# Seven products in place of eight for the pooling, gate, branch and output projections of a trunk layer

## The chip, the cores and the metric

The kernel runs on one core of a Trainium2 chip. The metric is device time in microseconds (us) of one execution; several executions are timed and their median is given. A hardware profile of one further execution gives the trace.

## The reference

One layer over 2048 latent tokens of width 1024, with 256 context tokens that serve as extra keys and values. All tensors are float32.

```python
q, k, v, p, gt = _split_proj(_modulate(x, sh1, sc1) @ w_in[l])   # 1024 q, 256 k, 256 v, 512 pool, 2048 gate columns
attn_o = _banded_attention(q, k, v, k_c, v_c, attn_sink[l])
# _merge_branches:
attn_d = attn_o @ w_ab                                           # 1024 x 1024
pooled = _multiscale_pool(p)                                     # centred means over 2/4/8/16 tokens, minus the token
pool_d = jnp.einsum('blgc,gcd->blgd', pooled, w_pool).reshape(B, L, D_MODEL) * pool_scale
merged = jax.nn.sigmoid(g_attn) * attn_d + jax.nn.sigmoid(g_pool) * pool_d
y = merged @ w_out                                               # 1024 x 1024
x = _layernorm(ALPHA * x + g1 * y, ln1_g[l], ln1_b[l])
u = _modulate(x, sh2, sc2)
h = jnp.square(jax.nn.relu(u @ w1)) @ w2                         # 1024 x 4096, 4096 x 1024
x = _layernorm(ALPHA * x + g2 * h, ln2_g[l], ln2_b[l])
```

## The kernel before

TensorE (PE) multiplies in a fast float32 format with fewer bits. A float32 operand is therefore split in two: ScalarE (ACT) casts the high part and VectorE (DVE) subtracts it to get the low part (`split`, two lines: L59 and L62). A product is three matmuls, high by high, high by low and low by high, so a tile of 512 columns costs three 128x512 matmuls for each 128 rows of depth.

The kernel has these stages, one after the other:

- **Attention**, to about 872 us: 64 units (16 blocks of 128 tokens, 4 key heads), with the q, k and v projections of later blocks filled in between. The modulated input `u` is spilled to DRAM (`u_scr`), the attention output to `a_scr`. In the last two blocks `early_pool` fills PE with two of the pooling projections.
- **The middle**, 872 to about 1762 us. The tokens are taken in two halves `c` of 1024. For each half come the pooling projections (`p_group`), the means (`p_finish`, `pool_gate`), the 16 gate tiles (`ps_gp`, `ps_ga`), the attention branch (`ps_ab`), the merge, the output projection (`out_mm`, `ps_out`, matmuls of 256 columns), the first layer norm and the transposes of the second input (`u2_half`). These products are plain: eight blocks of 128 depth, all columns. Gates, means and merged values stay in SBUF. `ada_next` spreads the late modulation vectors (`adacc`) over the first half.
- **MLP up**, 1762 to about 2390 us: 32 items (`Pair`), each 256 weight columns for 1024 tokens, computed by Strassen's scheme in its Winograd form: seven products (1, 6, 2, 7, 5, 4, 3) of 12 matmuls each, with sums of weight blocks on GpSimd (POOL), sums of the results on DVE from PSUM, and sums for the next product on POOL. The weight parts are split into `R` tiles seven steps ahead, in eight slots. The left operands (`La`, `Lb`) stay for 16 items.
- **MLP down**, 2390 us to the end, with seven products over the whole depth (`ps_y`).

PE's order is written out by hand (`tc.manual_schedule`); the other engines get their order from a scheduler that works through the program with its own estimates. All transfers are issued by SyncE's queue (SP), in order: a transfer that waits for its data holds up those behind it.

Of the kernel before, what the change touches and what calls it, by code (L numbers as in the profile page):

```python
# [36 lines left out]
def block_kernel(  # L37
# [7 lines left out]
    if u_scr is None:  # L45
        u_scr = tc.dram_tile([P, KT, T], F32, name="u_scr")
        a_scr = tc.dram_tile([P, KT, T], F32, name="a_scr")
    x1_scr = tc.dram_tile([T, D], F32, name="x1_scr")
    g2_scr = tc.dram_tile([D], F32, name="g2_scr")
    us_scr = [tc.dram_tile([P, 7, 4, 512], F32, name=f"us_scr{c}") for c in range(2)]  # L50
    hs_scr = [[tc.dram_tile([P, 4, 16, P], F32, name=f"hs_scr{c}{p}") for p in range(7)] for c in range(2)]
# [55 lines left out]
    rpx = ExitStack()  # L107
    rp = rpx.enter_context(sbuf("right", side="right"))
# [4 lines left out]
    def raw_tile(shape):  # L113
        return rp.tile(shape, F32, name="raw", tag="raw", bufs=2)
# [8 lines left out]
    wk = [(rp.tile([P, 4, 512], F32R, name="wkh", tag="raw", bufs=2), wkp.tile([P, 4, 512], F32R, name=f"wkl{h}"))  # L123
# [436 lines left out]
    UP = (0, 344, 688)  # L560

    def load_u(xs, u0, uu, pieces=1):

        def step(kk):
            raw = raw_tile([P, 2, UW])
            sp.dma_start(raw, u_scr[:, 2 * kk:2 * kk + 2, u0:u0 + UW])
            for k in range(2):
                uh = slot(xs, 0, [P, UW], F32R, "uh2")
                ul = slot(xs, 1, [P, UW], F32R, "ul2")
                for z in [slice(i, i + UW // pieces) for i in range(0, UW, UW // pieces)]:  # L570
                    split(uh[:, z], ul[:, z], raw[:, k, z])
                uu.append((uh, ul))
        return [lambda kk=kk: step(kk) for kk in range(4)]

    uu0 = []
    early = []

    def early_pool(g):

        def begin():  # L580
            raw = big.tile([P, KT, P], F32, name="w1", tag="x", bufs=1)
            sp.dma_start(raw, w_in_r[:, :, 1536 + g * P:1536 + (g + 1) * P])
            both = twp.tile([P, 2, KT, P], F32R, name="w1s", tag="w1s", bufs=1)
            w.extend((both[:, 0], both[:, 1]))
            split(*w, raw)
            pt = ptp.tile([P, PW], F32, name="pt1", tag="pt1", bufs=2)
            pool.memset(pt[:, 0:8], 0.0)
            early.append(pt)

        def step(i, k):  # L590
            if k == 0:
                box[i] = ps512("ps_p", "proj")[:, 0:344]
            wh, wl = w
            uh, ul = (t[:, UP[i]:UP[i] + 344] for t in uu0[k])
            pe.matmul(box[i], wh[:, k, :], uh, start=k == 0, stop=False)
            pe.matmul(box[i], wh[:, k, :], ul, start=False, stop=False)
            pe.matmul(box[i], wl[:, k, :], uh, start=False, stop=k == KT - 1)
            if k == KT - 1:
                act.copy(early[g][:, 8 + UP[i]:8 + UP[i] + 344], box[i])
        box, w = {}, []  # L600
        return [[begin]] + [u for i in range(3) for u in [[lambda i=i, k=k: step(i, k)] for k in range(KT)] + [[]]]
# [11 lines left out]
    for n, (b, g) in enumerate(order):  # L613
# [24 lines left out]
        if (b, g) == (NB - 3, 1):  # L638
            wkx.close()
            ptx = ExitStack()  # L640
            ptp = ptx.enter_context(sbuf("pooled", side="right"))
            twp = at.enter_context(sbuf("tailw", side="right"))
            lu = load_u(RA, 0, uu0, 3)
        if (b, g) == (NB - 3, 2):
            lu[0]()
# [79 lines left out]
    for c in range(2):  # L725
# [16 lines left out]
        if c:  # L742
            w_first = wcols(w_in, 1536)
# [225 lines left out]

# [344 lines left out]
```

## Time and profile before

| | before |
|---|---|
| median of 3 runs | 3038.16 us (3036.88 to 3038.42) |
| the profiled execution's own time | 3039.96 us |
| its span, first to last instruction | 3038.2 us |
| PE busy | 2909.0 us (96%) |
| DVE, ACT, POOL busy | 1819.1, 1369.1, 1380.6 us |
| bytes moved | 395.38 MB |

The busy share of PE is an average. The windows by stage and the waits are read first, the groups of instructions next: the first tell where PE stands idle, the second what one instruction of each kind takes. Matmuls overlap, so the time for one is the busy time of a group divided by its count, not the mean duration.

### The profile page before, as it was taken

What the parts mean: (1) busy time and instruction counts of PE and PEld (TensorE: products, weight loads), DVE (VectorE), ACT (ScalarE), POOL (GpSimd) and SP (SyncE); (2) the same over time, 40 slices, a digit from 0 to 9 for tenths busy, and PEclk for the clock granted to TensorE, in tenths of its full rate; (3) what the DMA queues carried; (4) which work ended last, traced back from release to release, by engine and by line L of the source; (5) the groups of instructions that cost most, each with busy time, mean ns of one, the idle gap of its engine ahead of it and who ended that gap; (6) DMA issues with size and microseconds to landing.
All of it is one profiled execution on the core that took longest, in us unless ns stands there. A gap on an engine that the chain in (4) does not pass through costs nothing. (4 is left out here: it accounts for less than half of the span.)

```text
span 3038.2 us, 42601 instructions
## 1 busy us (share of the span) xinstructions
PE 2909.0 (96%) x15336; PEld 2481.3 (82%) x15336; DVE 1819.1 (60%) x3201; ACT 1369.1 (45%) x2462; POOL 1380.6 (45%) x1638
## 2 busy tenths in 40 slices
PE   8899999999899999899999779999999799999998
PEld 5789989998888888888889668888888587888886
DVE  5577877877875444742144775557555453556675
ACT  3477767777741131432121455556555332333342
POOL 1867777777540014423032556657665240123244
PEclk9999999999999999999999889999999899999999
DMA  7111111112234433342122475547554684566563
GB/s 255 35 32 37 32 37 31 38 42 61 67 100 144 127 125 111 112 144 78 56 97 84 141 263 161 153 149 222 156 153 124 246 308 153 187 215 218 196 209 108
DMA packets 343015, 395.38 MB, mean 130 GB/s; under 512 B 16785, under 2 KB 277009, under 8 KB 341010
## 3 DMA queue, kind: packets, MB, share of 16 engines
q1 hardware_dynamic: 342802, 392.64, 40.5%
q8 instruction: 121, 1.98, 0.3%
q14 instruction: 92, 0.75, 0.1%
HBM read 275.13 MB, written 117.44 MB: 129 GB/s over the span
## 5 line engine op out<-in xcount | busy, mean ns | idle before, releaser
L1220 PE MATMUL ps_y<-La,R 128*128 128x512 f32 x2688 | 619.4, 393 | 25.8 <-ACT R L59 12.1
L1220 PEld LDWEIGHTS ps_y<-La,R 128*128 128x128 f32 x2688 | 508.9, 190 | 136.4 <-ACT La L59 13.7
L1039 PE MATMUL ps_h<-La,R 128*128 128x512 f32 x2112 | 485.2, 390 | 0.3 <-ACT cx L1044 0.3
L1039 PEld LDWEIGHTS ps_h<-La,R 128*128 128x128 f32 x2112 | 397.2, 188 | 83.3 <-ACT cx L1044 0.7
L62 DVE TENSOR_TENSOR R<-hraw,R 128x512 fp32r<-128x512 f32 x224 | 198.0, 890 | 150.7 <-ACT R L59 150.2
L59 ACT CAST R<-hraw 128x512 fp32r<-128x512 f32 x224 | 137.6, 621 | 281.3 <-PE ps_y L1220 272.9
L62 DVE TENSOR_TENSOR pl<-ps_pt,ph 128x512 fp32r<-128x512 f32 x312 | 212.5, 686 | 70.5 <-ACT ph L59 68.6
L465 POOL TENSOR_SCALAR s<-s,sm 128x640 f32<-128x640 f32 (+1 forms) x256 | 201.6, 795 | 103.0 <-DVE sm L464 53.9
L462 ACT ACTIVATE s<-s,sm 128x641 f32<-128x641 f32 (+1 forms) x256 | 209.8, 820 | 70.2 <-DVE sm L456 69.8
L456 DVE CUSTOM_DVE_ANT_0 s<-ps_s,mask,nsink 128x640 f32<-128x640 f32 (+1 forms) x256 | 211.5, 863 | 29.8 <-PE ps_s L451 29.7
L59 ACT CAST ph<-ps_pt 128x512 fp32r<-128x512 f32 x312 | 179.3, 580 | 109.3 <-PE ps_pt L486 106.0
L861 POOL TENSOR_TENSOR sa<-sa,m 128x512 f32<-128x512 f32 x32 | 57.1, 1805 | 374.5 <-DVE sa L860 374.5
L486 PE MATMUL ps_pt<-ident,s 128*128 128x128 f32 x1248 | 189.7, 274 | 12.4 <-DVE pl L62 8.2
L62 DVE TENSOR_TENSOR R<-sraw,R 128x512 fp32r<-128x512 f32 x160 | 146.3, 917 | 77.3 <-ACT R L59 76.8
L59 ACT CAST wh<-raw 128x2048 fp32r<-128x2048 f32 (+1 forms) x38 | 67.0, 1771 | 276.1 <-DMA raw<-w_in 73.6
L486 PEld LDWEIGHTS ps_pt<-ident,s 128*128 128x128 f32 x1248 | 151.6, 141 | 43.1 <-DVE pl L62 11.3
L62 DVE TENSOR_TENSOR wl<-raw,wh 128x2048 fp32r<-128x2048 f32 (+1 forms) x38 | 86.3, 2274 | 159.5 <-ACT wh L59 159.5
L59 ACT CAST R<-sraw 128x512 fp32r<-128x512 f32 x160 | 98.9, 621 | 155.2 <-PE ps_h L1039 97.5
L1039 PE MATMUL ps_h<-Lb,R 128*128 128x512 f32 x576 | 139.5, 396 | 25.4 <-ACT Lb L59 21.9
L1039 PEld LDWEIGHTS ps_h<-Lb,R 128*128 128x128 f32 x576 | 109.8, 191 | 49.7 <-ACT Lb L59 22.3
L66 PE MATMUL ps_out<-wh,mg 128*128 128x256 f32 x512 | 143.1, 281 | 0.0
L67 PE MATMUL ps_out<-wl,mg 128*128 128x256 f32 x512 | 142.8, 280 | 0.0
(264 smaller groups left out, 7098.4 us busy)
## 6 DMA issues: line engine op xcount, KB each, us to landing
hraw<-hs_scr SPq DMA_DIRECT2D x112, 512.0 KB, 4.0
w<-w_mlp_out SPq DMA_DIRECT2D x72, 512.0 KB, 5.4
sraw<-w_mlp_in SPq DMA_DIRECT2D x64, 512.0 KB, 6.3
hs_scr<-s SPq DMA_DIRECT2D x96, 256.0 KB, 4.6
raw<-w_in SPq DMA_DIRECT2D x19, 1024.0 KB, 5.5
raw<-w_ada SPq DMA_DIRECT2D x16, 1024.0 KB, 5.3
rw<-us_scr SPq DMA_DIRECT2D x14, 1024.0 KB, 5.4
raw<-u_scr SPq DMA_DIRECT2D x8, 1032.0 KB, 5.5
```

Source lines behind the costliest of these rows:

```text
L59: act.copy(hi, src)
L62: (lo_eng or dve).tensor_tensor(lo, src, hi.bitcast(F32), ALU.subtract)
L66: pe.matmul(ps, sh, mh, start=first, stop=False)
L67: pe.matmul(ps, sh, ml, start=False, stop=False)
L456: dve.tensor_tensor_reduce(out=s[:, 0:n], in0=pieces[z][2], in1=mk[z], op0=ALU.add, op1=ALU.min, scale=-1.0 / math.sqrt(HD), scalar=nsink[ ...
L462: act.activation(s[:, 0:n + 1], s[:, 0:n + 1], AF.Exp, bias=sm[:, 0, j:j + 1], scale=-1.0, accum_out=sm[:, 1, j:j + 1])
L465: pool.tensor_scalar(s[:, 0:n], s[:, 0:n], sm[:, 2, j:j + 1], 1.0, ALU.mult, ALU.mult)
L486: pe.transpose(pt[:, c:c + P], self.s.probs[2 * z + j][:, o:o + P], ident)
L861: pool.tensor_tensor(s, s, m0[j][:, a:a + m], ALU.add)
L1039: pe.matmul(ps, a, b, start=p in (1, 6, 5) and k == 0 and i == 0, stop=k == 3 and i == 2, skip_group_check=p not in (1, 6, 5))
L1220: pe.matmul(ps, a, b, start=n == 0 and z == 0, stop=n == 15 and z == 2)
```

## The change

The four projections of the middle are computed by the same seven products as the MLP. The two halves of the depth and the two halves of the tile's rows or columns are the blocks. Everything after attention is one stream of 68 items of seven products: 20 items of pooling and gate columns (10 for each half of the tokens), 8 of the branch (`BranchCols`), 8 of the output projection (`Rows`, one for 256 tokens) and 32 of the MLP up (`HiddenCols`). The MLP down stays as it is, but for the names of its buffers.

- Six items have their products 1 and 2 computed early, in the last two attention blocks (`Tail`, `NX = 6`), in place of `early_pool`.
- The sums of the left operand are made beside the stream as jobs: `act_sums` loads 1 MB, makes four sums and stores them (four times for each half of `u` and of `a`; on POOL for the first, on DVE for the other three). `w_out_planes` does it for the output weights. The means are 16 jobs of 512 tokens (`pool_job`).
- Gates, means and merged values no longer stay in SBUF: each result goes to DRAM (`p_scr`, `sa_scr`, `sp_scr`, `mp_scr`, `ms_scr`) and is loaded again. A branch tile loads its gate and its mean through a ring of three tiles (`ldring`), a left operand its raw planes through another ring of three (`rwring`).
- The first layer norm of the second half of the tokens (`ln1_late`) and the last four of the modulation sums run beside the first half of the MLP up.
- The `R` tiles are split five steps ahead, in six slots, where it was seven and eight.

```diff
-    UP = (0, 344, 688)
...
+    def act_sums(scr, sums, c, kk, e, raw, new):
+
+        sp.dma_start(raw, scr[:, 2 * kk:2 * kk + 2, c * CH:(c + 1) * CH])
+        v = raw.rearrange("p k (b r t) -> p k r b t", r=2, t=P)
+        a11, a12, a21, a22 = v[:, 0, 0], v[:, 1, 0], v[:, 0, 1], v[:, 1, 1]
+        s1, s2 = (new().rearrange("p (b t) -> p b t", t=P) for _ in range(2))
+        e.tensor_tensor(s1, a21, a22, ALU.add)
+        e.tensor_tensor(s2, s1, a11, ALU.subtract)
+        e.tensor_tensor(a21, a11, a21, ALU.subtract)
+        e.tensor_tensor(a12, a12, s2, ALU.subtract)
+        for p, t in ((5, s1), (6, s2), (7, a21), (3, a12)):
+            sp.dma_start(sums[c][:, SPL[p], kk].rearrange("p (b t) -> p b t", t=P), t)
...
-            pending += early_pool(0) + early_pool(1)
+            pending += tail.steps()
...
-    w_first = wcols(w_in, 1792, pieces=4)
...
-        if c == 0:
-            pooled = [p_finish(early[g], g) for g in range(2)]
-            for g in (2, 3):
-                pooled.append(p_finish(p_group(w_first, g), g))
...
+    rring = mpa.ring(6 * 4096, name="R")
+    rawring = mb.ring(3 * 8192, name="sraw")
+    rwring = mb.ring(3 * 2048, name="rw")
+    extring = mb.ring(4 * 2048, name="ext")
+    string = mb.ring(10 * 2048, name="st")
+    PQ = 512 + 16
+    ldring = gp_[0].ring(3 * 2048, name="ld")
+    pjring = gp_[0].ring(4 * PQ * 4, name="pj")
...
+            for k in range(4):
+                raw = rwring.tile([P, 512], F32, name="rw")
+                s = self.src(p)[:, k]
+                sp.dma_start(raw if len(s.shape) == 2 else blocks(raw), s)
+                t = ltile(p, k)
+                split(t[:, 0], t[:, 1], raw)
+                self.L[p].append(t)
...
+            ps = self.X if p in (1, 2) else self.Z if p in (5, 3) else self.Y
+            r = self.R.pop(p)
+            first = p in (1, 6, 5)
+            for k in range(4):
+                m = self.stage.L[p][k]
+                mm = ((r[:, 0, k], m[:, 0]), (r[:, 0, k], m[:, 1]), (r[:, 1, k], m[:, 0]))
...
+    class BranchCols(Cols):
...
+        def fin(self, key, ps, t):
+            r, h = rn(key)
+            s, m = ldtile("sa"), ldtile("mp")
+            sp.dma_start(blocks(s), tok_dst(sa_scr, 2 * self.n + h, self.c, r))
+            sp.dma_start(blocks(m), tok_dst(mp_scr, 2 * self.n + h, self.c, r))
+            if t is None:
+                t = sttile("c11")
+                dve.tensor_tensor(t, ps, s, ALU.mult)
+            else:
+                dve.tensor_tensor(t, ps, t, ALU.add)
+                dve.tensor_tensor(t, t, s, ALU.mult)
+            (dve if key in (11, 12) else pool).tensor_tensor(t, t, m, ALU.add)
+            combine(key, t, self.got, self.put)
...
+    for kk in range(4):
+        job(2 * kk, ada, kk)
+        job(2 * kk + 1, sums, u_scr, us1, 1, kk)
+        job(9 + kk, w_out_planes, kk)
+    for n, (z, g, q) in enumerate((z, g, 2 * z + q) for z in range(2) for g in range(4) for q in range(2)):
+        job(12 + n // 2, pool_job, g, q)
+    for kk in range(4):
+        job(13 + kk // 2 * 2, sums, a_scr, as1, 0, kk)
+        job(17 + kk // 2 * 2, sums, a_scr, as1, 1, kk)
+    for k in range(8):
+        job(8 + 2 * k, ada, 4 + k)
...
+    seq = [(p, i) for g in groups for p in ORDER for i in g if not (items[i].early and p in (1, 2))]
+    AHEAD = 5
...
+        items[i].prod(p)
+        if i + 1 in cuts:
+            items[i + 1].stage.fill(p)
+        if n + AHEAD < len(seq):
+            q, j = seq[n + AHEAD]
+            items[j].prep(q)
```

What the change does to the order is shown at two places of the branch stage. In the rows, `raw`, `sraw` and `rw` are loaded tiles; `R`, `La`, `av`, `mg` and `wl` are split parts; `sa` is a gate, `mp` a weighted mean; `c_`, `cx`, `cu`, `cv` are results of an item. SP's queue before, at the start of the first half's branch:

```order
L667 DMA raw<-w_in 128x8x256 [waits DMAHW5_49,DVE_49]
L667 DMA raw<-w_ab 128x8x256 [waits DMAHW7_49,DMAHW0_49,DVE_49]
L842 DMA raw<-a_scr 128x2x1024 [waits DMAHW6_49,DVE_49]
L842 DMA raw<-a_scr 128x2x1024 [waits DMAHW0_49,DVE_49]
L964 DMA g_scr<-gb_11461 1x1024 [waits DVE_49]
L842 DMA raw<-a_scr 128x2x1024 [waits DMAHW1_49,DVE_49]
```

SP's queue now, in the first half's branch:

```order
L930 DMA ms_scr_73<-cv 512x1x128 [waits Pool_49]
L935 DMA sa<-sa_scr 128x4x128 [waits DMAHW6_49,DMAHW3_49]
L936 DMA mp<-mp_scr 128x4x128 [waits DMAHW1_49,DVE_49]
L935 DMA sa<-sa_scr 128x4x128 [waits DMAHW7_49,DMAHW5_49,Pool_49]
L936 DMA mp<-mp_scr 128x4x128 [waits DMAHW3_49,DVE_49]
L930 DMA ms_scr_73<-s_15513 512x1x128 [waits Pool_49]
L847 DMA sraw<-w_ab 128x4x256 [waits DMAHW0_49,DVE_49]
L847 DMA sraw<-w_ab 128x4x256
L935 DMA sa<-sa_scr 128x4x128 [waits DMAHW4_49,DMAHW2_49,Pool_49]
L936 DMA mp<-mp_scr 128x4x128 [waits DMAHW5_49,DVE_49]
```

Loads of gates and means, loads of weights and stores of results now alternate on the one queue; a gate's load waits for the slot that POOL or DVE frees, and a store for its sum on POOL. DVE before, in the same stage:

```order
L62 TENSOR_TENSOR av<-raw,av 128x512 [waits Activation_49]
L62 TENSOR_TENSOR wl<-raw,wh 128x2048 [waits DMAHW6_49,Activation_49]
L860 TENSOR_TENSOR sa<-ps_ab,sa 128x512 [waits PE_49] x2
L62 TENSOR_TENSOR mg<-sa,mg 128x512 [waits Activation_49] x2
L860 TENSOR_TENSOR sa<-ps_ab,sa 128x512 [waits PE_49] x2
L62 TENSOR_TENSOR wl<-raw,wh 128x2048 [waits DMAHW7_49,Activation_49]
```

DVE now, in the second half's branch:

```order
L943 TENSOR_TENSOR c_16212<-c_16212,mp 128x512 [waits DMAHW2_49,DVE_49]
L68 TENSOR_TENSOR La<-rw,La 128x512 [waits DMAHW1_49,Activation_49]
L941 TENSOR_TENSOR cv<-ps_16259,cv 128x512 [waits PE_49]
L68 TENSOR_TENSOR R<-sraw,R 128x512 [waits Activation_49]
L942 TENSOR_TENSOR cv<-cv,sa 128x512 [waits DMAHW4_49,DVE_49]
L941 TENSOR_TENSOR cv<-ps_16283,cv 128x512 [waits PE_49]
L68 TENSOR_TENSOR R<-sraw,R 128x512 [waits DMAHW6_49,Activation_49]
L941 TENSOR_TENSOR cx<-ps_16137,cx 128x512 [waits PE_49]
L68 TENSOR_TENSOR La<-rw,La 128x512 [waits DMAHW0_49,Activation_49]
```

Sums from PSUM (`ps_`), low parts for the running item, low parts for the next stage and the gate's multiply now share DVE, and the multiply waits for a transfer.

## Rows read from the trace of the kernel before

**Rows 1.** The page: busy time by engine, and the span in 40 slices

```profile
PE 2909.0 (96%) x15336; PEld 2481.3 (82%) x15336; DVE 1819.1 (60%) x3201; ACT 1369.1 (45%) x2462; POOL 1380.6 (45%) x1638
PE   8899999999899999899999779999999799999998
DVE  5577877877875444742144775557555453556675
PEclk9999999999999999999999889999999899999999
DMA  7111111112234433342122475547554684566563
```

**Rows 2.** Windows by stage: length, busy time (count) by engine, clock, DMA share, GB/s

```profile
400.00:760.00 360.00, 358.77 (x2441) 326.65 (x2440) 288.16 (x671) 259.54 (x553) 273.60 (x530) 1.00 0.15 41
800.00:872.00 72.00, 68.84 (x527) 67.00 (x525) 50.22 (x120) 52.85 (x114) 31.44 (x56) 1.00 0.07 16
872.00:1762.00 890.00, 840.23 (x4544) 725.16 (x4544) 431.82 (x743) 237.19 (x344) 241.11 (x169) 0.97 0.36 118
1762.00:2390.00 628.00, 614.39 (x2688) 506.99 (x2688) 357.75 (x409) 331.37 (x537) 373.35 (x251) 0.99 0.54 165
2390.00:2420.00 30.00, 19.12 (x55) 13.07 (x56) 16.95 (x20) 15.79 (x21) 0.39 (x1) 0.72 1.03 396
```

**Rows 3.** Waits of PE, longest first: us in total, times, longest

```profile
PE ps_h L1039 <- ACT Lb L59: 21.9, 1, 21.9
PE ps_y L1220 <- ACT R L59: 12.1, 1, 12.1
...
PE ps_u L929 <- ACT xn L900: 11.2, 3, 5.0
```

**Rows 4.** Groups of PE matmuls: shape, count | busy us, mean ns | idle before

```profile
L1220 PE MATMUL ps_y<-La,R 128*128 128x512 f32 x2688 | 619.4, 393 | 25.8 <-ACT R L59 12.1 <-ACT La L59 11.3 <-DVE La L62 2.3
...
L66 PE MATMUL ps_out<-wh,mg 128*128 128x256 f32 x512 | 143.1, 281 | 0.0
...
L685 PE MATMUL ps_gp<-uh,wh 128*128 128x512 f32 x256 | 102.2, 399 | 0.0
...
L685 PE MATMUL ps_p<-uh,wh 128*128 128x344 f32 x144 | 44.6, 334 | 3.2 <-ACT wh L59 1.7 <-ACT uh L59 1.5
...
L929 PE MATMUL ps_u<-ident,xn 128*128 128x128 f32 x128 | 25.0, 330 | 20.6 <-ACT xn L900 11.2 <-ACT u2f L930 9.3
...
L595 PE MATMUL ps_p<-uh,w1s 128*128 128x344 f32 x48 | 15.9, 332 | 0.0
```

**Rows 5.** DVE in order of time in the MLP up: start us, duration us

```profile
1798.57 0.68 DVE L1057 TENSOR_TENSOR cv<-ps_h,cv 128x512 f32<-128x512 f32 x1
1799.17 1.18 DVE L62 TENSOR_TENSOR R<-sraw,R 128x512 fp32r<-128x512 f32 x1
1800.27 0.68 DVE L1057 TENSOR_TENSOR cv<-ps_h,cv 128x512 f32<-128x512 f32 x1
1800.87 1.18 DVE L62 TENSOR_TENSOR R<-sraw,R 128x512 fp32r<-128x512 f32 x1
```

**Rows 6.** POOL in order of time, the same stretch

```profile
1798.06 1.74 POOL L1020 TENSOR_TENSOR sraw<-sraw,ext 128x512 f32<-128x512 f32 x1
1799.76 1.74 POOL L1010 TENSOR_TENSOR ext<-sraw,ext 128x512 f32<-128x512 f32 x1
```

**Rows 7.** POOL's sums of weight blocks in the MLP up: min/median/max ns

```profile
L1010 POOL TENSOR_TENSOR ext<-sraw,ext x29: 1277/1287/1752, 1799.8 to 2317.1; 128x512 f32<-128x512 f32 x29
```

**Rows 8.** DMA issues: count, KB each, median us from issue to landing

```profile
hs_scr<-s SPq DMA_DIRECT2D x96, 256.0 KB, 4.6
...
adaw<-w_ada SPq DMA_DIRECT2D x16, 512.0 KB, 8.1
...
x<-x_scr SPq DMA_DIRECT2D x32, 256.0 KB, 3.7
```

More of the change, by code (lines that the diff above doesn't have):

```diff
@@ L575, in block_kernel @@
[L575 to L601, printed above, removed]
+    ORDER = (1, 6, 2, 7, 5, 4, 3)
@@ new lines, in block_kernel @@
+    items = []
+    w_ab_v, w1v = weight_cols(w_ab), weight_cols(w_mlp_in)
+    for c in range(2):
+        stage = Stage(act_planes(u_scr, us1, c), tail.L if c == 0 else None)
+        for i in (0, 1, 2, 3, 4, 5, 6, 7, 8, 9) if c == 0 else (0, 1, 6, 7, 8, 9, 2, 3, 4, 5):
+            it = (PoolCols if i < 2 else GateCols)(stage, c, i, w_in_v, U_COLS[i])
+            it.early = c == 0 and i < NX
+            if i >= 2:
+                it.g, it.dst = (i - 2) % 4, sa_scr if i < 6 else sp_scr
+            items.append(it)
@@ new lines, in block_kernel @@
+    job(20, lambda: tc.keep_in_program_order(act.preload_act_table_set(EXP_LN)))
+    job(28, to_rows)
+    for z in range(4):
+        job(37 + 2 * z, ln1_late, 4 + z)
+        job(46 + 2 * z, ada, 12 + z)
+    cuts = [i for i in range(1, len(items)) if items[i].stage is not items[i - 1].stage]
+    groups, i = [], 0
+    while i < len(items):
+        two = i + 1 < len(items) and items[i].stage is items[i + 1].stage and (i == 0 or i in cuts or i + 2 in cuts)
+        groups.append(list(range(i, i + 1 + two)))
+        i += 1 + two
@@ new lines, in block_kernel @@
+    seq = [(p, i) for g in groups for p in ORDER for i in g if not (items[i].early and p in (1, 2))]
+    AHEAD = 5
+    items[0].load()
+    items[1].load()
+    items[0].stage.fill(6)
+    for n in range(AHEAD):
+        p, i = seq[n]
+        items[i].prep(p)
+        items[0].stage.fill(p)
+    for p in ORDER:
+        items[0].stage.fill(p)
+    at_step = {}
+    for g in groups:
+        steps = [n for n, (_, i) in enumerate(seq) if i in g]
+        for z, i in enumerate(g):
+            at_step.setdefault(steps[z * len(steps) // len(g)], []).append(i)
@@ new lines, in block_kernel @@
+    for i in (0, 1):
+        items[i].begin()
+    for n, (p, i) in enumerate(seq):
+        for f in [f for d, f in ends if d == 0]:
+            f()
+        ends[:] = [(d - 1, f) for d, f in ends if d]
+        for j in at_step.get(n, ()):
+            ahead = [g for g in groups if g[0] == j + 1]
+            for i2 in ahead[0] if ahead else ():
+                items[i2].load()
+                items[i2].begin()
+            for f in jobs.get(j, ()):
+                f()
+        items[i].prod(p)
[4 more added lines that the diff above has]
+            items[j].prep(q)
```

875 lines of the change are left out of this document (459 added, 416 removed).

## The prediction

> **What bounds the kernel now.** I read the page's busy line first, then windows by stage, then PE's waits, then single rows for prices. PE is busy 2909.0 of 3038.2 us [rows 1], so time is PE's work plus the little it waits. By stage [rows 2]: the end of attention is full (68.84 of 72 us), the middle has 840.2 of 890, the MLP up 614.4 of 628. The long waits are single events at stage starts: 21.9 and 12.1 us, and 11.2 in three [rows 3]. The other engines have room in the middle: DVE 432 of 890, ACT 237, POOL 241, DMA share 0.36 at 118 GB/s. So fewer matmuls there come off the time one for one, until something else fills: the question is what the change asks of DMA and DVE in a shorter middle.
>
> **What PE saves.** A 512-column matmul costs 619.4/2688 = 0.2304 us [rows 4]. In units of that, the middle had 3 x 768 = 2304 for the gates and the branch (one group of 256 of the nine stands in [rows 4]), 432 pooling matmuls of 344 columns = 290, and 1536 output matmuls of 256 columns = 768 (one group of three stands for each): 3362, or 775 us. Now there are 240 products: six items with five, 14 gate items with seven, 16 branch and output items with seven. At 12 matmuls each that is 2880, or 664 us. Saved: 111. Half of the 128 transposes `ps_u` (25.0 us, [rows 4]) leaves for the MLP up: 12 more. If nothing but PE limits the stream, the middle's length S is 840 - 111 - 12 = 717 us.
>
> **What is added outside the middle.**
> - End of attention: 6 items x 2 products x 12 = 144 matmuls of 512 columns replace 144 of 344 (three groups of 48, one stands in [rows 4]). That is 144 x 0.2304 x (1 - 344/512) = 11 us, and it counts, since PE is full there. The 16 sums on POOL (16 x 1.287 = 21 us, [rows 7]) hide under POOL's 31 of 72 [rows 2]; without that cover they would cost up to 21.
> - Opening of the stream: its first weight loads stand on SP behind attention's last stores, then come a load (3.7 to 8.1 us, [rows 8]), two POOL sums and a split. I take 12 us, nearest to load plus sums plus split. Bounds: 2, were it prefetched, and 21.9, the longest stage start of [rows 3].
> - MLP up: four pieces of layer norm, half the transposes, four modulation pieces, and `R` five steps ahead instead of seven. The transposes are 12 us of PE, but 13.6 us of idle in that stage (628 - 614.4) takes part of it: +8, bounds 0 and 25 (twice the transposes). MLP down: 0, its matmuls and rings keep their sizes.
>
> **What the middle now asks of DMA.** Gates, means, merged values and the sums of the operands go through DRAM. By the shapes of the diff, in MB: weights, gate stores and early reloads of the 20 items 43; sums of `u` 8 and of `a` 17; output-weight planes 12; pooling jobs 22; modulation weights 13; branch 40 (8 items x 1.05 of weights, 8 loads and 7 stores of 0.262); output items 39 with `us2`; 152 left tiles of 0.262, 40. Together 233 before rounding, where the middle moved 118 GB/s x 890 us = 105. The rate at full share is worked out from two windows of [rows 2]: 165/0.54 = 306 GB/s in the MLP up, 396/1.03 = 384 at the start of the MLP down. I take 306, because its transfers are 128x512 tiles and weight pieces like the new ones. Then 233 MB need 761 us, and 607 at the other rate. The load is uneven: the first 28 items carry all but the output items' 46 MB, so 187 MB, or 611 us at 306. PE works there 184 products x 12 x 0.2304 = 509, with `ps_pd` and starts some 536. The stream is thus 75 us longer than PE alone: 792. SP's single queue also alternates stores that wait for sums with loads that wait for slots, so DMA won't be full all the time; 13 us for that is my estimate (one turn like the 12.1 of [rows 3]). **S = 805**; bounds 717 and 930 (below).
>
> The Trainium skill ("DMA: Bandwidth & Descriptors", section Specifications) gives HBM about 358 GB/s for one core. By it 233 MB would be an estimated 651 us, under PE's 717, and the sum would be rival B's. The trace has 396 GB/s in one window, above that figure, and 306 per full share in the other, below it.
>
> **What it asks of DVE and POOL.** DVE starts 512-column operations 0.60 us apart (1798.57 to 1799.17, [rows 5]). The middle has some 876 of that size (240 low parts of `R`, 152 of the left tiles, 196 sums from PSUM, 64 merge operations, 112 for norm and sums, 32 for the output weights, 80 for the means): 526 us, with modulation (38) and short chains (16) 580. POOL has about 245 operations' worth of 1.287 us. A DVE operation with two SBUF operands takes 1.18 beside them and 0.68 for one that reads PSUM [rows 5], and POOL's own go from 1.287 [rows 7] to 1.74 [rows 6]. Charging 0.50 to DVE for each POOL operation gives 122: 702 of 717. That leaves DVE no room, but it isn't the longest. A gain on DVE is excluded: its 580 stand against 432 before. ACT's casts number like DVE's low parts, against 237 of 890 busy.
>
> **The sum.** 3038.2 - 890 + 11 + 12 + 8 + S = 2179.2 + 805 = 2984. The profiled execution's own time was 3039.96, 1.8 above its span; the median of the runs, 3038.16, equals the span within 0.1, so the sum on the span is taken for the median. It equals the time before at S = 859.
>
> **Rivals.**
> - **B, PE keeps pace.** DMA runs near 384 per share, 607 us in all, and the queue stays full. S is 717 to 745, so 2896 to 2924. For it: the stage order gives each stage's inputs several items of lead, and 396 GB/s was seen at share 1.03 [rows 2]. Against: no long stretch before ran over a share of 0.54.
> - **C, the rings of three set the pace: slower than before.** A branch item takes eight gate and mean loads through three slots, 2.67 turns; a turn is the landing (3.7 to 8.1 us, [rows 8]) plus about 1.7 of use (POOL's 1.74, [rows 6]). At 3.7 that is 14.4 us and hides under the item's 7 x 12 x 0.2304 = 19.4; at 8.1 it is 26.1, or 6.8 x 8 items = 54 us. It decides from a landing of 5.5 us. The left tiles: 28 at a stage change, three slots, a turn of 8.1 + 1.3 = 9.4 makes 88 us, where a product's turn comes 26 steps (72 us) after its first load: 16 at each of five changes, 80. From PE's 717 and DMA's 75 with one or both, S is 870 to 930: 3049 to 3109. For it: landings go up with share, and these loads queue behind stores. Against: two of the three rows of [rows 8] lie below 5.5.
> - **D, DVE and POOL exclude each other wholly.** Then DVE's 580 and POOL's 216 large operations, 216 x 1.287 = 278 plus 30 of short ones, add up: S = 888, time 3067. For it: in [rows 5] every low part pays, and both engines are long at the same moment. Against: it pays 0.50, not a whole operation. The Trainium skill ("SBUF — State Buffer", section Who interferes with whom) states that a DVE instruction with two SBUF inputs and a GpSimd instruction that reads SBUF exclude each other for a whole instruction. By that rule D is the outcome; the trace agrees that they collide, and shows 0.50 of 1.287 as the price.
> - **E, in between.** A partial C on top of the forecast, S 853 to 865: within 0.2% of before.
>
> That the change does nothing isn't open: the matmuls are fewer.
>
> **How the numbers follow.** The forecast (DMA sets the pace of the first 28 items, S 771 to 851, 2950 to 3030) has 0.45, B 0.17, C 0.22, D 0.05, E 0.09; 0.02 is for faster yet. A difference of 0.2% (6 us) is about what a measurement of this kernel can tell. Faster: 0.45 + 0.17 + 0.01 = 0.63; same 0.09; slower 0.22 + 0.05 + 0.01 = 0.28. The range runs from the middle of B, 2905, to the middle of C and all of D, 3080; about 0.2 is left outside. The forecast's own range is 2950 to 3030.
>
> **What would show it.** PE's total busy time about 100 us less, whatever else. The stream from attention to the MLP up near 805 us, with a DMA share of 0.8 to 0.95 in the pooling, gate and branch items, PE busy 85 to 90% there, and its waits traced back to loads of weights. An opening gap of about 12 us; the MLP up near 636. PE at 96% in the stream would show B. C: DVE or POOL waiting for `sa`, `mp` or `rw` while the DMA share is well under 0.8. D: DVE over 95% busy, with low parts at 1.2 us and more in most rows. The prediction is wrong at its base if the 233 MB land at well over 306 GB/s, or if the output items, where DMA has least to do, are slow too.

## The result and the profile after

The changed kernel takes 3443.89 us (median of 4 runs, 3439.97 to 3448.51) beside 3038.29 for the kernel before in the same session: a ratio of 1.134, with a 95% interval of 1.132 to 1.136. It is 406 us slower, where 2984 was forecast. That is 460 above the forecast, and outside its range.

From the page of after, the rows that answer to [rows 1]: busy time by engine, and PE, DVE, clock and DMA in 40 slices.

```profile
PE 2925.9 (85%) x13944; PEld 2393.3 (70%) x13944; DVE 2166.7 (63%) x3757; ACT 1601.8 (47%) x2947; POOL 1551.5 (45%) x1858
...
PE   8899999999698767578835866679899988999998
...
DVE  4687887877666755779844654436754453455676
...
PEclk9999999999899878789967878889999989999999
DMA  6111111116767866768934644456655395454553
```

PE executes 1392 matmuls fewer and is busy longer, 2925.9 us for 2909.0. From slice 11 to slice 27 it mostly stands at 50 to 80%, and the granted clock drops in the same slices. Another engine or DMA is near full there only around the end of the branch: DVE in slice 19 and DMA in slice 20. Windows of after by stage answer to [rows 2] (length, then PE, PEld, DVE, ACT and POOL busy with counts, granted clock, DMA share, GB/s): items 0 to 9, items 10 to 19, branch, output rows, first and second half of the MLP up, MLP down.

```profile
892.00:1097.00 205.00, 179.46 (x711) 139.59 (x712) 142.63 (x211) 76.23 (x131) 70.79 (x48) 0.92 0.74 232
1097.00:1463.00 366.00, 250.13 (x955) 192.88 (x954) 233.54 (x333) 101.84 (x175) 108.36 (x86) 0.82 0.71 228
1463.00:1673.00 210.00, 173.13 (x683) 138.02 (x682) 172.17 (x203) 61.84 (x108) 99.45 (x63) 0.89 0.79 243
1673.00:1966.00 293.00, 178.54 (x735) 141.48 (x734) 161.04 (x314) 123.27 (x203) 76.17 (x98) 0.78 0.52 171
1966.00:2420.00 454.00, 345.65 (x1418) 273.81 (x1417) 228.60 (x377) 219.30 (x376) 216.48 (x198) 0.86 0.52 158
2420.00:2749.00 329.00, 316.50 (x1346) 255.39 (x1345) 177.36 (x218) 161.44 (x272) 185.05 (x129) 0.98 0.51 149
2749.00:3443.00 694.00, 639.98 (x2688) 513.15 (x2688) 395.52 (x585) 262.93 (x426) 182.41 (x100) 0.96 0.57 198
```

Matmuls alone would need 160 us in the first window (58 products x 12 x 0.2304), 194 in the second, 155 in the third and fourth, 310 in each half of the MLP up. So the loss is in items 10 to 19 (+172), the output rows (+138) and the first half of the MLP up (+144), with 45 and 55 in the first and third windows, 19 in the second half of the MLP up and 46 in the MLP down, which took 648 before. PE's waits (us in total, times, longest) say what was waited for there; before, the longest waits of this kind [rows 3] were 11.2 us in three:

```profile
PE ps_u L1002 <- ACT u2q L1004: 174.5, 32, 9.6
PE ps_pd L72 <- ACT ph L65: 56.8, 5, 20.6
PE ps_ar L1100 <- DVE adacc L1082: 44.4, 4, 11.9
PE ps L814 <- DVE cu L824: 36.6, 10, 6.1
...
PE ps_pd L72 <- DVE spl L1169: 24.3, 12, 5.4
PE ps_u L1002 <- ACT c L991: 23.2, 1, 23.2
```

The 5568 matmuls of the products (`ps`, L814) aren't the ones that wait most. It is three small kinds: the transposes of the second input (`ps_u`, 198 us in these two rows), the pooling products of the means (`ps_pd`, 81) and the sums of the modulation (`ps_ar`, 44), together 323. PE takes its instructions in their written order, so each of them holds up the products behind it. What each one waits for is called its chain below: a load, sums, a split and a store that follow one another through a small buffer.

**One such wait, step by step.** Four times for each pair of rows, PE transposes a group into PSUM, ACT writes it to `u2q`, POOL makes four sums in it, and SP stores it. There is one `u2q`. Rows of after in order of time (start, duration, operation, in brackets the idle time before it and its releaser):

```profile
2105.13 0.45 POOL L1010 TENSOR_TENSOR u2q<-u2q 128x128 f32<-128x128 f32 x1
2105.61 13.83 SPq L1011 DMA_DIRECT2D us<-u2q  x3
2108.76 0.56 ACT L1004 ACTIVATE u2q<-ps_u,mod 128x256 f32<-128x256 f32 x1 [8.39 <-DMA us<-u2q]
2109.38 0.71 PEld L1002 LDWEIGHTS ps_u<-ident,sraw 128*128 128x128 f32 x4 [9.63 <-ACT u2q L1004]
2109.38 1.11 PE L1002 MATMUL ps_u<-ident,sraw 128*128 128x128 f32 x4 [9.40 <-ACT u2q L1004]
...
2116.02 1.12 PE L1002 MATMUL ps_u<-ident,sraw 128*128 128x128 f32 x4 [5.52 <-ACT u2q L1004]
```

ACT waits 8.39 us for the store to land, and PE 9.40 for ACT. The next group comes 6.64 us later (2109.38 to 2116.02), with 1.1 us of PE work in it. One turn of the buffer is two ACT operations, four sums and a store of some 3 us. Eight pairs pay about 22 us each.

**What the clock adds.** Two of the pooling matmuls in after, one just after such a wait and one after matmuls without a pause:

```profile
1206.06 0.80 PE L73 MATMUL ps_pd<-ph,wp 128*128 128x512 f32 x1
...
1249.85 0.40 PE L73 MATMUL ps_pd<-ph,wp 128*128 128x512 f32 x1
```

The granted clock is 0.64 in the 9 us around the first and 1.00 in the 7 us around the second. After a stretch of idle PE runs at its lower level, 1.2 GHz, and the same matmul takes twice as long. That is the larger part of how fewer matmuls came to more busy time.

### The profile page after: what moved, and what is told of

It is laid out like the page before. It is cut to its first block, busy times and chain, and to the rows that moved or that the text cites. A ratio compares the mean times of both kernels' runs of the same rounds, so it can differ in the third digit from the quotient of the medians.

```text
span 3443.0 us, 42738 instructions
## 1 busy us (share of the span) xinstructions
PE 2925.9 (85%) x13944; PEld 2393.3 (70%) x13944; DVE 2166.7 (63%) x3757; ACT 1601.8 (47%) x2947; POOL 1551.5 (45%) x1858
## 5 line engine op out<-in xcount | busy, mean ns | idle before, releaser
L814 PE MATMUL ps<-La,R 128*128 128x512 f32 x5568 | 1373.1, 409 | 101.2 <-DVE cu L824 36.6
L814 PEld LDWEIGHTS ps<-La,R 128*128 128x128 f32 x5568 | 1091.9, 197 | 374.2 <-DVE cu L824 27.8
L65 ACT CAST R<-sraw 128x512 fp32r<-128x512 f32 x344 | 212.3, 619 | 376.0 <-PE ps L814 300.9
L68 DVE TENSOR_TENSOR R<-sraw,R 128x512 fp32r<-128x512 f32 x344 | 298.1, 868 | 117.1 <-ACT R L65 114.5
L855 POOL TENSOR_TENSOR ext<-sraw 128x512 f32<-128x512 f32 x60 | 83.9, 1399 | 425.6 <-DVE R L68 148.1
L68 DVE TENSOR_TENSOR La<-rw,La 128x512 fp32r<-128x512 f32 x180 | 165.5, 936 | 31.7 <-ACT La L65 31.1
L65 ACT CAST La<-rw 128x512 fp32r<-128x512 f32 x180 | 109.4, 619 | 145.1 <-DMA rw<-us 58.1
L68 DVE TENSOR_TENSOR R<-ext,R 128x512 fp32r<-128x512 f32 x120 | 111.1, 926 | 65.1 <-ACT R L65 64.7
L510 PE MATMUL ps_o<-ph,vring 128*128 128x256 f32 x368 | 117.3, 334 | 3.1 <-ACT o L519 3.1
L867 POOL TENSOR_TENSOR sraw<-sraw,ext 128x512 f32<-128x512 f32 x60 | 86.6, 1443 | 72.7 <-DVE R L68 72.0
```

The source lines that it names most:

```text
L65: act.copy(hi, src)
L68: (lo_eng or dve).tensor_tensor(lo, src, hi.bitcast(F32), ALU.subtract)
L510: pe.matmul(self.po[:, z * 256:(z + 1) * 256], v, self.p[u][w][:, x * 256:(x + 1) * 256], start=w == 0 and mine[0] == (z, i), stop=w == 1 ...
L814: pe.matmul(ps, a, b, start=first and k == 0 and i == 0, stop=k == 3 and i == 2, skip_group_check=not first)
L855: pool.tensor_tensor(self.op[5], b12, b11, ALU.subtract)
L867: pool.tensor_tensor(self.b[0], self.b[2], self.op[6], ALU.subtract)
```

## The experiments

All edits are on the changed kernel unless said otherwise; a time is compared with its 3444. Each time is of one execution, but for the last run, which has four; the four of the changed kernel lie within 9 us, so a difference of a few us says nothing. The table gives the stretches in us, measured on the products' first matmuls in each trace; "alone" is products x 12 x 0.2304.

| stretch | alone | after | spread transposes | one mean job | no means | no side matmuls | three edits | no chains |
|---|---|---|---|---|---|---|---|---|
| items 0 to 9 | 160 | 204 | 205 | 214 | 204 | 194 | 201 | 194 |
| items 10 to 19 | 194 | 367 | 366 | 284 | 240 | 228 | 232 | 225 |
| branch | 155 | 210 | 210 | 233 | 208 | 295 | 277 | 217 |
| output rows | 155 | 293 | 264 | 294 | 297 | 237 | 242 | 195 |
| MLP up, first half | 310 | 454 | 421 | 442 | 447 | 379 | 374 | 360 |
| MLP up, second half | 310 | 329 | 329 | 328 | 327 | 323 | 323 | 324 |
| MLP down | | 694 | 694 | 695 | 689 | 693 | 691 | 692 |
| time | | 3444 | 3381 | 3384 | 3306 | 3238 | 3237 | 3097 |

Two theories stood against each other. Theory W (later called theory chain): PE stands behind small side work that waits for its own chain. Theory M: bytes and SP's queue pace the middle, as the prediction had it, and the waits only show where.

### The transposes two products apart

```diff
...
-                ends.append((8, lambda: turn_pair(self.n, (self.z[11], self.z[12]), (self.z[21], self.z[22]))))
+                for kp in range(4):
+                    ends.append((4 + 2 * kp, lambda kp=kp: turn_pair(self.n, (self.z[11], self.z[12]), (self.z[21], self.z[22]), (kp,))))
...
-        ends.append((9, lambda: turn_pair(i, ts[0], ts[1])))
+        for kp in range(4):
+            ends.append((6 + 2 * kp, lambda kp=kp: turn_pair(i, ts[0], ts[1], (kp,))))
```

> The four groups of transposes of a pair of rows are put two products apart (4, 6, 8, 10 products after the pair's last one, where all four came at once after 8), so that the single buffer u2q is stored while PE multiplies. Theory W (PE stands in line behind the small matmuls of the side work, each of which waits for its own chain): PE's 201 us of waits at ps_u fall below 60, the granted clock of that stretch rises above 0.9, and the time falls by 150 to 230, to 3215 to 3295. Theory M (the middle is paced by DMA and SP's queue, the waits only show where): the waits move to the products or their weights, and the time falls by less than 60, above 3380.

Measured: 3380.5, 63 us less. PE's waits in this run:

```profile
PE ps_u L1002 <- ACT u2q L1004: 69.2, 32, 6.5
...
PE ps_u L1002 <- ACT sraw L991: 36.0, 5, 14.0
...
PE ps_u L1002 <- ACT c L991: 33.0, 3, 28.3
```

The wait for `u2q` fell by 105 us. Some 43 of that came back as waits for the layer norm, which now isn't ready when the first transposes come (`c` and `sraw`, 69 us for 26). Theory W missed: PE's waits at `ps_u` are still 138 us where it said under 60, and the time lies 85 us above its range. Theory M is missed by little (63 us gained where it said under 60). So the wait is real, but moving the matmuls earlier exposed the next link. Two buffers for `u2q` weren't tried: they need 4 KB in each partition where 1 KB is free.

### One job of means for each item

```diff
-        z = q // 2
+        z = q
...
-    for n, (z, g, q) in enumerate((z, g, 2 * z + q) for z in range(2) for g in range(4) for q in range(2)):
-        job(12 + n // 2, pool_job, g, q)
+    for q in range(4):
+        for g in range(4):
+            job(8 + 4 * q + g, pool_job, g, q)
```

> One job of means for each item from 8 to 23, where it was two for each item from 12 to 19, so the second job no longer waits for the ring that the first one holds. Theory W: PE's 81 us of waits at ps_pd fall below 25, the items 10 to 19 take 280 us or less, where they took 366, and the time falls by 70 to 130. Theory M: those items move as many bytes as before at a share that was 0.71, the waits reappear elsewhere, and the time falls by less than 30.

Measured: 3384.4, 59 less, between the two theories (70 to 130, and under 30). Items 10 to 19 took 284 us for 367, just above the 280 of theory W. But 23 us came back in the branch, where four of the 16 jobs now lie, and 10 in items 0 to 9, and PE's waits at `ps_pd` fell only from 81 to 60, where under 25 was said.

### No jobs of means at all

```diff
-            sp.dma_start(blocks(m), tok_dst(mp_scr, 2 * self.n + h, self.c, r))
+            sp.dma_start(blocks(m), tok_dst(sp_scr, 2 * self.n + h, self.c, r))
...
-    for n, (z, g, q) in enumerate((z, g, 2 * z + q) for z in range(2) for g in range(4) for q in range(2)):
-        job(12 + n // 2, pool_job, g, q)
```

> Leaves out the 16 jobs of means with their loads, sums, pooling matmuls and stores; the branch loads the pooling gate in place of the mean, so its own loads stay. Theory chain (the jobs hand one ring of four units on from one to the next, and PE stands behind them): the items 10 to 19 take 215 to 260 us, where they took 367, and the time is 3290 to 3340. Theory M (bytes set the pace): 22 MB less, or 72 us at 306 GB/s, are the most that can be had: 3370 to 3444.

Measured: 3305.9, 138 less; items 10 to 19 took 240 us. Both lie in theory W's range, and the gain is nearly twice the 72 that the bytes could explain. The means cost 127 us in these ten items.

### No small matmuls on PE

`pe.transpose` in `turn_pair`, `mm3` in `pool_job` and `pe.matmul` in `ada` are left out; ACT and DVE read the transposes' input, `ph` and `acc` directly.

> Leaves out the small matmuls of the side work on PE: the transposes of the second input, the pooling products and the modulation sums; ACT and DVE read other SBUF tiles in their place, and every load, sum and store stays. Theory W: PE waits less than 120 us in the stream and its clock is above 0.93; the stream of 68 items takes 1250 to 1330 us where it took 1857, the time is 2850 to 2950. Theory M: the first 28 items stay above 720 us (they took 781), and the time is above 3150.

Measured: 3238.2, 206 less. Theory W missed by 290 us in the time. Theory M's time came (above 3150), and its first 28 items took 717 us where it said above 720; its reason fails in the runs with more bytes below. The wait had moved: the branch went from 210 to 295, with one wait of PE of 80.9 us for `cu`, a sum on DVE, from 1392 to 1473 us. What stood ahead of it was on POOL. POOL's rows in that stretch, the DVE operation that PE waited for, PE's row, and windows of the wait:

```profile
1399.68 1.35 POOL L943 TENSOR_TENSOR cx<-cx,mp 128x512 f32<-128x512 f32 x1 [1.48 <-DMA mp<-mp_scr]
...
1423.24 1.06 POOL L1146 TENSOR_TENSOR pt<-pt 128x527 f32<-128x527 f32 x1 [17.55 <-DMA pt<-p_scr]
1424.38 2.20 POOL L1150 TENSOR_TENSOR pt<-pt 128x525 f32<-128x525 f32 x2
...
1432.00 1.06 POOL L1146 TENSOR_TENSOR pt<-pt 128x527 f32<-128x527 f32 x1 [3.05 <-DMA pt<-p_scr]
1433.14 2.20 POOL L1150 TENSOR_TENSOR pt<-pt 128x525 f32<-128x525 f32 x2
1448.36 1.06 POOL L1146 TENSOR_TENSOR pt<-pt 128x527 f32<-128x527 f32 x1 [13.02 <-DMA pt<-p_scr]
...
1465.60 1.26 POOL L912 TENSOR_TENSOR s<-cx,cv 128x512 f32<-128x512 f32 x1 [2.55 <-DVE ph L68]
```

```profile
1472.20 0.69 DVE L824 TENSOR_TENSOR cu<-ps,cx 128x512 f32<-128x512 f32 x1 [0.85 <-DMA ms_scr<-cx]
```

```profile
1472.94 3.35 PE L814 MATMUL ps<-La,R 128*128 128x512 f32 x7 [80.94 <-DVE cu L824]
```

```profile
1395.00:1415.00 20.00, 0.00 (x0) 0.00 (x0) 14.53 (x22) 5.47 (x9) 6.68 (x5) 0.50 1.00 311
1415.00:1435.00 20.00, 0.00 (x0) 0.00 (x0) 4.17 (x7) 1.02 (x2) 6.13 (x7) 0.50 0.40 132
1435.00:1455.00 20.00, 0.00 (x0) 0.00 (x0) 5.41 (x10) 1.64 (x3) 4.79 (x5) 0.50 0.35 112
```

In the first 20 us of the wait DMA is full (1.00); after them it isn't, and the wait goes on. Two jobs of means take 25.1 us (1423.24 to 1448.36), with 3 to 5 us of POOL work in each and DMA at a share of 0.35 to 0.40. A job takes three of the four units of its ring (`pjring`), so the next job's load can't start until the last one's parts are split, or its results stored. The branch's sums (L912, L914) stand behind these jobs in POOL's order; the second one's result is stored (`ms_scr<-cx`), the store frees a slot, `cu` needs the slot, and PE needs `cu`. That PE's queue was freed only moved the head of the line to POOL's. The first sum depends on the jobs in a second way: in the branch its own buffer comes from `pjring` too (`stile` in the kernel), and what released it last is the split of a job (`ph`).

The Trainium skill ("PSUM — Partial Sum Buffer", section Engine vs sequencer instructions) states that the queues of ScalarE, VectorE and GpSimdE are strict FIFO and that matmuls start in program order. These rows agree with it as far as they go: the last of the sum's inputs, `cx`, was written at 1401, while POOL stood idle 17.55 and 13.02 us for the jobs' loads. They don't tell POOL's order from the shared ring, since either would hold the sum back.

### Three edits together

The run without side matmuls, with one mean job for each item and a pad of 32 bytes (below).

> Three edits together: the small matmuls of the side work left out as in the run without them, one job of means for each item, and the pad of 32 bytes. What is left is the 464 products with all loads and stores. Theory chain: without the chains in PE's line and with the jobs of means spread, the branch's 196 us fall to below 110, the stream takes 1400 to 1500 us, the time is 2970 to 3080. Theory M: the first 28 items stay above 660 us, the time is above 3120.

Measured: 3236.5, no better than without the second and third edit. Theory W missed again, by 156 us in the time, and the branch still took 277. Both bounds of theory M were met (first 28 items 710 us, above 660; time above 3120). A reading that keeps theory W is that PE runs ahead of the jobs until it needs their results, and then goes at their pace; the next run tests it.

### No chains

Jobs of means, `turn_pair` and the small matmuls are all left out; the branch loads `sp_scr` for the mean, and the MLP up loads `wo_scr` for `us2`, so the products keep their loads.

```diff
...
-                ends.append((8, lambda: turn_pair(self.n, (self.z[11], self.z[12]), (self.z[21], self.z[22]))))
+                pass
...
-        stage = Stage(lambda p, c=c: us2[c][:, POS[p]])
+        stage = Stage(lambda p: wo_scr[:, POS[p]])
...
```

> Leaves out all three chains: the jobs of means, the second input's transposes with their buffer u2q, their sums and stores, and the small matmuls of the modulation; the branch loads the pooling gate and the MLP up the output-weight planes in their place, so the products keep all their loads. Sums, norm, gates and modulation on DVE stay. Theory chain (whatever waits behind a slow chain in an in-order queue, PE's or POOL's, is what is lost): the branch falls from 277 us in the run with three edits to 160 to 200, rows and MLP up from 940 to 790 to 840, time 2980 to 3070. Theory M (bytes and SP's queue pace the first 28 items): these stay above 640 us, and the time above 3120.

Measured: 3097.1, 347 less. Theory M missed: the first 28 items took 636 us, under its 640 by little, and the time is 23 below its 3120. Theory W missed too: the time is 27 us above its range, with the branch at 217, and rows and MLP up at 880, both above what it said. So the chains hold most of the loss, and some 60 us over before remain without them. This run also does less work (82 us of small matmuls, 37 MB of transfers), so 347 is an upper bound for the chains' waits alone.

### More bytes

Every gate result is stored a second time, to a tensor that nobody reads (60 stores, 15.7 MB), once in the changed kernel, once in the one without chains.

```diff
...
             sp.dma_start(tok_dst(self.dst, 2 * self.g + h, self.c, r), blocks(t))
+            sp.dma_start(tok_dst(extra_scr, 2 * self.g + h, self.c if self.dst is sa_scr else 2 + self.c, r), blocks(t))
```

> Each result of a gate item is stored a second time, to a tensor that nobody reads: 58 stores of 0.262 MB, 15 MB, or 50 us at 306 GB/s. Theory chain: DMA has room at a share of 0.7, the time rises by 0 to 15 us. Theory M: it rises by 35 to 60 us.

> The kernel without the three chains, with each gate result stored a second time: 58 stores of 0.262 MB, 15 MB, 50 us at 306 GB/s, in the first 20 items. Theory bytes (DMA paces the gate items once the chains are gone, as the prediction had it): these 20 items, 419 us, grow by 25 to 55 us. Theory latency (DMA has room there, single waits pace them): they grow by less than 12.

Measured: 3459.1, or 15 more, in the changed kernel (all of it in items 0 to 9, none in items 10 to 19; theory M had said 35 to 60), and 3092.3 without chains, where 3097.1 was the time without the stores. Windows of items 0 to 9 and 10 to 19, first without chains, then with the added stores:

```profile
888.00:1082.00 194.00, 173.01 (x698) 134.20 (x698) 130.14 (x194) 70.28 (x119) 61.05 (x43) 0.96 0.73 225
1082.00:1307.00 225.00, 204.17 (x841) 161.76 (x841) 163.78 (x234) 81.96 (x143) 56.95 (x40) 0.96 0.78 247
```

```profile
887.00:1089.00 202.00, 176.24 (x695) 136.62 (x695) 131.79 (x192) 70.08 (x119) 60.40 (x43) 0.93 0.80 242
1089.00:1304.00 215.00, 199.97 (x843) 160.22 (x842) 168.74 (x236) 82.21 (x144) 58.41 (x40) 0.97 0.95 300
```

In items 10 to 19 the DMA share goes from 0.78 to 0.95, and they take 215 us where they took 225; items 0 to 9 take 203 for 194. Together that is 418 us for 419, where bytes as the pace would have added 25 to 55. So bytes don't pace these 20 items, even there, and theory M falls as far as it speaks of bytes, although three runs met its bounds for the time (no side matmuls, three edits, and the last one below). Its other half, SP's one queue, was not tested apart from the chains.

### Where an operand begins

In the trace of before, matmuls with 512 columns follow each other at 226.7 ns. In after three of an item's seven products do that, and in the other four they follow at 231 to 238. Those four products (1, 2, 6, 7) have their left tiles, which are the moving operand, in the pools on the right side of SBUF. These tiles begin 224 bytes past a multiple of 256; the others, and those of the MLP before, begin 64 past one. A pad in front moves them: 32 bytes to 192 past, 160 bytes to 64 past.

```diff
+    ctx.enter_context(sbuf("pad", side="right")).tile([P, 40], F32, name="pad")
     rp = ctx.enter_context(sbuf("right", side="right"))
```

> A pad of 32 bytes in front of the right-hand pools, nothing else: the 16 left tiles of products 1, 2, 6 and 7 then begin at a multiple of 64 bytes, as all of before's left tiles do; in the changed kernel they begin 32 bytes off. In its trace matmuls follow each other at 226.7 ns in three of the seven products of an item and at 231 to 238 in four; in before all at 226.7. Theory start address: all at 226.7, the stream 15 to 25 us and the MLP down 10 to 16 us shorter, time 3400 to 3420. Rival (other traffic in SBUF slows PE): the two speeds stay, time within 8 us of 3444.

> A pad of 160 bytes in place of 32, nothing else: the right-hand left tiles then begin 64 bytes past a multiple of 256, as all of before's left tiles and the changed kernel's fast ones do (with 32 bytes they were 192 past, in the changed kernel 224). Theory offset within 256 bytes: matmuls of products 1, 2, 6 and 7 follow at 226.7 ns, not 233, time 3400 to 3420. Rival (it is the place in SBUF, far from the weights, not the offset): they stay at 233, time 3436 to 3448.

Measured: 3441.8 with 32 bytes (2 less, as the rival had it), 3424.1 with 160 (20 less, 4 above the range of the offset theory, whose pace came as it said). The theory that a multiple of 64 is what counts fell. Windows of 150 us with PE full, in the MLP down of after, with 32 bytes, with 160 bytes, and of before; the first count is PE's matmuls:

```profile
2930.00:3080.00 150.00, 150.00 (x649) 121.73 (x648) 80.00 (x114) 50.84 (x86) 23.60 (x12) 1.00 0.52 183
```

```profile
2930.00:3080.00 150.00, 150.00 (x650) 121.82 (x649) 81.39 (x116) 50.80 (x87) 23.71 (x12) 1.00 0.55 188
```

```profile
2930.00:3080.00 150.00, 150.00 (x662) 123.90 (x661) 86.30 (x118) 51.25 (x87) 26.24 (x13) 1.00 0.56 196
```

```profile
2600.00:2750.00 150.00, 150.00 (x664) 124.20 (x663) 75.62 (x94) 41.59 (x63) 30.46 (x14) 1.00 0.55 179
```

649, 650, 662, 664: with the pad of 160 the pace of before is back. The MLP down went from 694 to 683. In the stream most of the gain was lost in waits (1857 to 1849).

### The hidden sums in halves

On the kernel with the pad of 160 bytes:

```diff
-    hring = m2p.ring(2 * 8192, name="hraw")
+    hring = m2p.ring(3 * 4096, name="hraw")
...
-        raw = hring.tile([P, 16, P], F32, name="hraw")
-        sp.dma_start(raw, hs_scr[i // 4][p][:, i % 4])
+        for z in range(2):
+            raw = hring.tile([P, 8, P], F32, name="hraw")
+            sp.dma_start(raw, hs_scr[i // 4][p][:, i % 4, 8 * z:8 * z + 8])
```

> On the kernel with the pad of 160 bytes, the MLP down loads its hidden sums in pieces of 512 KB through three buffers, as before, in place of 1 MB through two. Theory queue (a load of 1 MB waits on SP's queue for its buffer, up to 10.8 us, with the weight loads behind it): the weights come in time, the waits of PE at La fall, and the MLP down goes from 683 to 660 to 672 us, the time from 3424 to 3401 to 3413. Rival (the late weights come from elsewhere): within 6 us of 3424.

Measured: 3410.5, 14 less, which lies in the range for the time (3401 to 3413). But only 8 of it is in the MLP down (683 to 675), less than the 11 that were the least expected; the other 6 came where nothing was changed. Between the runs that don't touch the MLP down it varies from 689 to 695, so 8 is little above that. SP's longest wait for a buffer and PE's waits for left tiles, with the pad alone and then with halves:

```profile
SPq L1322 <- DVE R L68: 236.9, 39, 10.5
...
PE ps_y L1378 <- ACT La L65: 27.8, 6, 6.1
```

```profile
SPq L1324 <- DVE R L68: 255.4, 80, 6.4
...
PE ps_y L1379 <- ACT La L65: 20.8, 6, 6.4
```

The direction is that of the queue theory, the size isn't. Of the 46 us lost in the MLP down, some 27 stay unsettled.

### Mended

The first two edits together, then with three more: the mean's gate tile from the ring of gates, `ps_ar` two products later, the late rows' transposes up to two products later, and the pad of 160 bytes.

```diff
...
-                m = pjtile("spl")
+                m = ldtile("spl")
...
-        ends.append((11, end))
+        ends.append((13, end))
...
```

> The spread transposes and the single mean jobs together. Theory W: the gains add, 3444 falls to 3080 to 3200. Theory M: above 3330.

> The spread transposes and single mean jobs, and beside them: the mean's gate tile from the ring of three that gates and means use later (so a job gives its ring back once its parts are split), the modulation's sum on PE two products later, the late rows' transposes two products later, and the pad of 160 bytes. Theory chain: PE's waits at ps_pd, ps_ar and ps_u, 234 us with the two edits alone, fall below 130; the time falls from 3314 to 3170 to 3250. Theory M: above 3290. Neither expects it below before.

Measured: 3314.1 for the two, 130 less, so their gains add (63 + 59); 3301.5 for all (3293.9 to 3310.2, 4 runs), a ratio to before of 1.088 (1.085 to 1.090). Both missed theory W's ranges (3080 to 3200, 3170 to 3250). The first lies 16 below theory M's bound of 3330, the second above its 3290. PE's waits in the last:

```profile
PE ps_u L1003 <- ACT u2q L1005: 83.6, 32, 8.2
PE ps_u L1003 <- ACT c L992: 34.0, 3, 28.7
...
PE ps_pd L72 <- DVE spl L1172: 31.0, 3, 18.3
PE ps_pd L72 <- DVE mod L1105: 22.9, 5, 14.7
```

The waits at the small matmuls are still 239 us, under other releasers, where 234 with the two edits alone were to fall below 130. Another place in the order moved these waits and did not take them away.

## Why the prediction was wrong, step by step

**The opening, and the end of attention: right.** The stream's first product starts at 892 us, where 872 + 11 + 12 = 895 was forecast; its longest wait there, 14 us, is within the bounds of 2 and 21.9.

**What PE saves: right as a count, wrong in us.** The matmuls are as many as counted. But PE's busy time rose by 17 where "about 100 less, whatever else" was said. The 5568 matmuls of the stream were busy 1373 us, 0.2466 each, not the 0.2304 of [rows 4]. That is 90 us: some 67 of it from 336 matmuls that follow each other at 0.43 us where the granted clock is at its lower level, some 20 from the operand's start. The sum took the price of a matmul as fixed and had no term for what a wait does to the work behind it.

**DMA: the loads right, their effect wrong.** From the windows, the middle moved 232 MB (232 x 205 + 228 x 366 + 243 x 210 + 171 x 293, in GB/s and us); 233 was the estimate. A share of 1.00 gave 311 GB/s (20 us in the run without side matmuls), and 0.95 gave 300, so 306 at full share was fair for these transfers. But "The stream is thus 75 us longer than PE alone" set the pace by bytes, and 15.7 MB more cost nothing once the chains were gone. The stretch of 28 items is 636 us without chains, near the 611 of the forecast, but not because of bytes: with the added stores it is 638. That nearness is luck.

**DVE and POOL: right.** The middle's four windows add up to 709 us of DVE, 702 was the estimate, and it was spread over 1074, so over the middle it wasn't the bound; its fullest stage is the branch, with 172 of 210. Rival D, with DVE over 95% busy, did not come. But the argument against it, that an operation pays 0.50 us and not a whole operation, misread the rows: both low parts of [rows 5] end 0.55 us after a POOL operation of [rows 6] ends (1800.35 after 1799.80, 1802.05 after 1801.50), as if each had waited for the rest of that operation. In the MLP up before, 90 of the 213 low parts of `R` take over 1 us, and each of the 90 ends 0.55 us after the end of a POOL operation that was running when it began. D's sum still isn't what bound the stream: DVE, whose busy time holds these waits, was busy 709 of 1074 us.

**The step that failed** is the middle's length as the larger of sums: S was PE's work or DMA's time, plus 13 us for a queue that isn't full all the time. Side work was entered as so many megabytes and so much busy time ("pooling jobs 22" MB, "short chains (16)" us of DVE), each under the cover of an idle engine. It has latency as well, and a ring that lets one job in at a time. At 12.6 us for a job of means, as in the run without side matmuls while PE stood still, 16 of them need 201 us; they were given eight items of 19.4, 155. In the changed kernel itself they followed each other at 18.8 us (14 jobs from 1198 to 1443 us). A turn of `u2q` is 6.6 us, for which PE was given none. Both could have been estimated from the rows of before: a landing of 3.7 to 4.6 us [rows 8], sums of about 1.3 [rows 7]. In place of the 805 came 1074, and in place of 636 for the MLP up came 783, since four of the eight pairs of rows lie there. These two make 416 of the 460; most of the rest is the 46 of the MLP down.

**Rival C had the mechanism and the wrong rings.** It said slower by short rings, 3049 to 3109 with 0.22; the measured time is still 335 above that. It priced the gates' and means' ring of three and the left tiles' ring. Issues of after (count, KB, median us from issue to landing) show the landings that it asked for:

```profile
sa<-sa_scr SPq DMA_DIRECT2D x32, 256.0 KB, 4.7
mp<-mp_scr SPq DMA_DIRECT2D x32, 256.0 KB, 4.4
```

Both are under the 5.5 us from which it decides. The rings that decided, `pjring` (four units, three for a job, and the branch's own sums take theirs from it) and `u2q` (one), were in the change and not looked at. The Trainium skill's figure of 358 GB/s ("DMA: Bandwidth & Descriptors", section Specifications), by which rival B would follow, had no part in it: the stages of the middle moved 171 to 243 GB/s, and PE didn't keep pace for another cause.

**MLP down at nothing: wrong by 46.** "Its matmuls and rings keep their sizes" wasn't so. It loads its hidden sums in pieces of 1 MB instead of 512 KB, and 16 of its 22 left tiles lie on the right side. 11 us went with the operand's start, some 8 with the pieces.

**What stays open.** Without the chains 3097 remains, 60 above before, with a clock of 0.88 to 0.96 up to the MLP up; up to 34 of it would be the start offset and the pieces (20 and 14 in the changed kernel, not run here), and for the rest the traces show many waits of a few us at `cu`, `cx` and `R` and no single owner; the branch holds the longest, 18.8 us for `cu`, at a DMA share of 0.89. How much of the chains' cost goes through SP's one queue stays open too: SP's longest waits, those for `La`, are 125 us in the stream of after and 123 without the chains, but its waits for `u2q`, 127 us, went with the chains.

## What to carry to other kernels

A sum of busy times and bytes is a floor. For each piece of side work that a main stream waits for, write down its turn (load, operations, store, through its smallest buffer), times how often, against the time that its place in the order allows; what is over is paid on every in-order queue that it stands in, and again in the clock. Taking the piece off one queue helps less than hoped while it heads another, or holds a ring that others draw on.

## What the runs showed of the hardware that was not expected

- The same matmul follows the last at 226.7 ns with its moving operand beginning 64 bytes past a multiple of 256, and at 233 to 235 on average with 192 or 224 past. In the MLP down, with 2688 matmuls, it is 11 us. Whether the offset counts by itself or against that of the weights, most of which begin 64 past, wasn't tried.
- A DMA share of 0.95 at 300 GB/s beside a PE at 93% did not make items 10 to 19 longer (215 us with it, 225 at 0.78).
- A low part on DVE, with two operands in SBUF, that begins while POOL works ends 0.55 us after that POOL operation (all 90 low parts of `R` over 1 us in the MLP up before); beside an idle POOL it takes 0.69 us.
